# Shifting the start of the product operands inside their slots, in the last feed-forward sub-layer of a diffusion backbone

## The chip, the cores and the metric

The kernel runs on one core of one Trainium2 chip. The metric is the device time of one execution in microseconds, the median of several runs; less is better.

## The reference

The reference is a small diffusion backbone of two layers over 512 latent tokens and 256 context tokens, with a model width of 1024. Each layer is a half-step SwiGLU feed-forward, a token mixer (a short gated convolution in layer 0, grouped-query attention in layer 1), and a second half-step SwiGLU. Every sub-layer starts with an RMSNorm with learned scale and shift and ends in a gated residual. Behind the attention only the latent tokens are still needed, so the last feed-forward sees 512 tokens:

```python
def swiglu(h, w_in, w_out):          # w_in: 1024 x 5632, w_out: 2816 x 1024
    gate, up = jnp.split(h @ w_in, 2, axis=-1)
    return (jax.nn.silu(gate) * up) @ w_out

h = norm_modulate(x_lat, norm_g[i, 2], m_lat[:, 2, 0], m_lat[:, 2, 1])
x_lat = x_lat + 0.5 * m_lat[:, 2, 2] * swiglu(h, ffn_w_in[i, 1], ffn_w_out[i, 1])
...
return rms_norm(x_lat, final_g)
```

## The kernel before

**Arithmetic.** All large products run on TensorE in the type fp32r (four bytes to an element). To keep float32 accuracy every operand is split into a high part, a rounded copy that ScalarE writes, and a low part, the rest, that VectorE writes (`split`, L189 to L191). A product of two operands is then three matmuls, in `mm3` (L863 to L866): weight high by operand high, weight high by operand low, weight low by operand high. Each has its own weight load.

**The first half of a feed-forward.** For each of the 22 chunks of 128 hidden columns, `gate` and `up` are computed from the weights of both (two 128-column blocks, each with its 1024 rows cut in two) and from the normed activations, cut in two over their 1024 rows and in two over their tokens (B11, B21, B12, B22: first index the rows, second the tokens). The first two chunks are computed directly. The other 20 use a scheme with seven products in place of eight (M1 to M7, `PRODUCTS`, L65), which needs sums of the weight blocks and of the operands; the operand sums are T1, T2, T3 and T4. So there are seven operand pairs, each made once for the sub-layer and read by 20 chunks:

```python
PRODUCTS = {"M1": ("A11", "B11", "A"), "M2": ("A12", "B21", "B"), "M3": ("S4", "B22", "C"), "M4": ("A22", "T4", "A"),
            "M5": ("S1", "T1", "C"), "M6": ("S2", "T2", "A"), "M7": ("S3", "T3", "A")}
```

A product is 4 steps over the rows by 3 matmuls, 12 matmuls in all (`product`, L1122 to L1132). In the last sub-layer each half has 256 tokens, so a matmul has 256 columns; in the first three feed-forward and convolution sub-layers it has 384, and the second half of a feed-forward (the operands gh and gl) works on 512. In the round of a chunk the order is M1, M2, M7 of the chunk before, M5, M6, M4 and M3 of the chunk before (`product_order`, L119 to L124), and TensorE follows the order of the program.

**Where the operands lie.** Fourteen slots, tags T0 to T13, are laid out once (`SLOT_ORDER`, L71; L593 to L595). A slot is as large as the largest tile that ever uses its tag: 6144 bytes in a partition (4 x 384 elements), and 6176 for slots 4, 5, 8 and 9, which in the first sub-layers hold B12 and B22 with two more columns. `t_tiles` (L736) puts the high and low part of an operand into two slots, from the first byte of each. In the last sub-layer the slots come from `LAST_T_SLOTS` (L74); B12 and T4 use the same two, one after the other. A tile there is 4 x 256 elements, 4096 bytes, so a part of the slot stays free.

**Where the weights lie.** A weight granule is one tile of 4096 bytes, high part in its first half and low part in its second; eight of them take turns (`place`, L254 to L267). The addresses that the program assigns are these: the granules begin at 96 modulo 256 bytes, the low parts as well; slots 0 to 3, 6 to 8 and 10 to 13 begin at 96, slot 9 at 128, slot 4 at 160, slot 5 at 192 modulo 256.

**Who makes the weights.** Weight blocks come by DMA into raw tiles. For a product, VectorE forms the sum of blocks where one is needed (L374, L383), ScalarE and VectorE split it into a granule (L190, L191), ahead of TensorE as long as granules are free.

Of the kernel before, what the change touches and what calls it, by code (L numbers as in the profile page):

```python
# [26 lines left out]
NH = NT // 2  # L27
# [44 lines left out]
HELD_AFTER_T = ((6, 7), (10, 11), (8, 9))  # L72

LAST_T_SLOTS = {"B11": (0, 1), "B21": (2, 3), "B12": (6, 7), "T4": (6, 7), "T1": (8, 13), "B22": (9, 10), "T2": (11, 12), "T3": (4, 5)}  # L74
LAST_F_SLOTS = {(0, 0): 4, (1, 0): 5, (0, 1): 11, (1, 1): 12}
HELD_AFTER_LAST_T = ((8, 13), (11, 12), (9, 10))
HELD_AFTER_HEADS = ((6, 7), (9, 10))
# [53 lines left out]
def backbone(ctx: ExitStack, tc: tile.TileContext, a: dict, out: bass.AP):  # L131
# [30 lines left out]
    vec, at = {}, 0  # L162
# [23 lines left out]
    def slot(n, shape, name, dt=F32R):  # L186
        return xp.tile([P, *shape], dt, name=name, tag=f"T{n}")
# [410 lines left out]
    hh, hl = [None] * KC, [None] * KC  # L598
# [125 lines left out]
    T, full = {}, {}  # L724
    geo = SimpleNamespace(tokens=TOKENS, half=NH, groups=BOTH, t_slots=T_SLOTS, f_slots=F_SLOTS)
# [8 lines left out]
        region.pop().close()  # L734

    def t_tiles(name, more=0):  # L736
        T[name] = [slot(n, [4, geo.half + more], f"t{name}{z}") for n, z in zip(geo.t_slots[name], "hl")]

    def t_split(name, src, ks, pinned=False):
        split(T[name][0][:, ks], T[name][1][:, ks], src[:, ks], pinned)  # L740
# [12 lines left out]
    def opening(i, s):  # L753
# [27 lines left out]
        def early(half):  # L781

            t_tiles(f"B{half + 1}1")
            off, n = geo.tokens[0]
            for k, (hi, lo) in enumerate(zip(*([t[:, k, :] for k in range(4)] for t in T[f"B{half + 1}1"]))):
                m = 4 * half + k
                scale = scl[:, m, LAT : LAT + 1]
                act.activation(hi, xs(m, off, n), AF.Copy, scale=scale)  # L788
                dve.scalar_tensor_tensor(out=lo, in0=xs(m, off, n), scalar=scale, in1=hi.bitcast(F32), op0=ALU.mult, op1=ALU.subtract)  # L789
# [6 lines left out]
        def parted(half, tok, p, which="both", more=0):  # L796
            name = f"B{half + 1}{tok + 1}"
            if p == 0 and which != "lo":
                t_tiles(name, more)
            hi, lo = T[name][0][:, PAIRS[p], : geo.half], T[name][1][:, PAIRS[p], : geo.half]  # L800
            src = full[half, tok][:, PAIRS[p]]
            if which != "lo":
                act.activation(hi, src, AF.Copy)
            if which != "hi":
                dve.tensor_tensor(out=lo, in0=src, in1=hi.bitcast(F32), op=ALU.subtract)
# [20 lines left out]
        def sum_parted(which, p, pinned=False):  # L826
            if p == 0:
                t_tiles(which)
            t_split(which, full[which] if which in full else full[0, 0], PAIRS[p], pinned)
# [984 lines left out]
    with tc.tile_pool(name="g1", bufs=1) as gp:  # L1814
        stage["ssq"] = lambda: gp.tile([P, NT], F32, name="ssq", tag="ssq")
        heads = attention(gp, 1, 1)
    geo.__dict__.update(tokens=HALVES, half=NL // 2, groups=((0, NL),), t_slots=LAST_T_SLOTS, f_slots=LAST_F_SLOTS)
    op4 = opening(1, 2)
# [79 lines left out]
```

## Time and profile before

| | |
|---|---|
| median of three runs | 2401.55 us (2401.49 to 2401.75) |
| the profiled execution: its own time, its span | 2401.78 us, 2399.9 us |
| granted TensorE clock, mean | 0.999 |
| TensorE matmuls | 14303, busy 99% of the span |
| VectorE, ScalarE | busy 85% and 49% |
| last feed-forward, first half and projections | about 2045 to 2390 us of the span |

Times are microseconds from the start of the span unless marked ns. PE is TensorE's matmul, PEld its weight load, DVE VectorE, ACT ScalarE, POOL GpSimd. L864 to L866 are the three lines of `mm3`, so a matmul is known by its tiles: `ps_A<-tT4h,w` is a matmul into an accumulator of tag A with the high part of T4 as the moving operand and a granule as the weights. Matmuls overlap in the record, and a duration of one is its latency; how fast they follow one another is read from their starts.

### The profile page before, as it was taken

The numbers are of one execution on the slowest core, as the hardware profiler recorded it, in microseconds if no ns is written. First come the engines' busy times: TensorE is split into PE (matmuls) and PEld (weight loads), VectorE is DVE, ScalarE is ACT, GpSimd is POOL, SyncE is SP. The second block draws the span as 40 slices with busy tenths as digits, with TensorE's granted clock in tenths as the row PEclk, the third lists the DMA queues.
The fourth block names the chain that finished last, engine by engine and source line by source line (L and its number), as shares of the span: only waits on it lengthen the run. The fifth ranks groups of instructions, "written<-read, shape, count | busy, mean of one in ns | idle before, by whom it ended". The sixth has DMA issues, their size and how long they took to land.

```text
span 2399.9 us, 37639 instructions
## 1 busy us (share of the span) xinstructions
PE 2379.0 (99%) x14303; PEld 2253.2 (94%) x14303; DVE 2032.3 (85%) x4018; ACT 1166.2 (49%) x2198; POOL 135.4 (6%) x256
## 2 busy tenths in 40 slices
PE   9999999999999999999999999999999999999998
PEld 6999999999999999999999999999998889999998
DVE  6989989978988888888877988788778987987777
ACT  5634334355535553443435544343355776555555
POOL 0001111100000001000000001101100000000000
PEclk9999999999999999999999999999999999999999
DMA  9234334430334123323432144443441101133231
GB/s 338 85 113 140 128 126 132 128 115 27 106 106 132 39 69 116 120 94 118 128 106 67 50 131 128 141 138 122 137 132 54 45 10 58 67 122 95 101 106 62
DMA packets 93062, 253.71 MB, mean 106 GB/s; under 512 B 10320, under 2 KB 18640, under 8 KB 92880
## 3 DMA queue, kind: packets, MB, share of 16 engines
q1 hardware_dynamic: 71984, 183.65, 23.3%
q0 software_dynamic: 20352, 67.12, 8.9%
q8 instruction: 112, 1.84, 0.3%
q14 instruction: 70, 0.57, 0.1%
q10 hardware_dynamic: 544, 0.52, 0.1%
HBM read 249.16 MB, written 2.10 MB: 105 GB/s over the span
## 4 chain that ended last, share of the span: by engine, by line
PE 92%; DVE 3%; ACT 3%; DMA 1%; issue 1%; SPq 0%; DVEq 0%; ACTq 0%
PE ps_A L864 16%; PE ps_A L865 16%; PE ps_A L866 16%; PE ps_C L865 11%; PE ps_C L866 11%; PE ps_C L864 11%; PE ps_B L866 3%; PE ps_B L864 3%; PE ps_B L865 3%; PE ps_T L1545 1%; DMA ada<-in_ada_w 0%; DVE f L766 0%; DMA raw<-in_ffn_w_in 0%; ACT pr L1528 0%; PE ps_O L866 0%
## 5 line engine op out<-in xcount | busy, mean ns | idle before, releaser
L190 ACT ACTIVATE w<-raw 128x512 fp32r<-128x512 f32 (+1 forms) x862 | 522.7, 620 | 716.7 <-PE ps_A L866 224.4
L191 DVE TENSOR_TENSOR w<-raw,w 128x512 fp32r<-128x512 f32 (+1 forms) x862 | 574.1, 679 | 120.0 <-ACT w L190 105.6
L510 POOL DMA_DIRECT2D aw<-in_ada_t x240 | 129.4, 539 | 1368.4 <-DVE mods L531 1100.1
L374 DVE TENSOR_TENSOR raw<-raw,raw 128x512 f32<-128x512 f32 x264 | 181.4, 689 | 8.1 <-DMA raw<-in_ffn_w_in 3.8
L865 PE MATMUL ps_C<-gl,w 128*128 128x512 f32 (+1 forms) x548 | 188.3, 344 | 0.0
L864 PE MATMUL ps_C<-gh,w 128*128 128x512 f32 (+1 forms) x548 | 188.2, 343 | 0.0
L866 PE MATMUL ps_C<-gh,w 128*128 128x512 f32 (+1 forms) x548 | 188.0, 343 | 0.0
L864 PE MATMUL ps_A<-gh,w 128*128 128x512 f32 (+1 forms) x540 | 185.5, 343 | 0.6 <-DVE x L932 0.6
L865 PE MATMUL ps_A<-gl,w 128*128 128x512 f32 (+1 forms) x540 | 185.5, 343 | 0.0
L866 PE MATMUL ps_A<-gh,w 128*128 128x512 f32 (+1 forms) x540 | 185.3, 343 | 0.0
L531 DVE CUSTOM_DVE_ANT_0 ps_S<-aw,silu_row,packed 128x512 f32<-128x512 f32 x208 | 156.9, 754 | 2.2 <-DMA aw<-in_ada_t 0.7
L531 DVE CUSTOM_DVE_ANT_0 ps_S<-aw,silu_row,mods 128x512 f32<-128x512 f32 x208 | 156.8, 754 | 1.0
L932 DVE SCALAR_TENSOR_TENSOR x<-ps_C,gat,x 128x512 f32<-128x512 f32 (+1 forms) x158 | 99.6, 631 | 43.6 <-PE ps_C L866 43.2
L864 PE MATMUL ps_A<-tB11h,w 128*128 128x384 f32 (+1 forms) x400 | 129.9, 325 | 0.2 <-ACT tB11h L788 0.2
L865 PE MATMUL ps_A<-tB11l,w 128*128 128x384 f32 (+1 forms) x400 | 129.5, 324 | 0.2 <-DVE tB11l L789 0.2
L866 PE MATMUL ps_A<-tB11h,w 128*128 128x384 f32 (+1 forms) x400 | 129.3, 323 | 0.0
L865 PE MATMUL ps_C<-tB22l,w 128*128 128x384 f32 (+2 forms) x376 | 121.7, 324 | 0.0
L866 PE MATMUL ps_C<-tB22h,w 128*128 128x384 f32 (+2 forms) x376 | 121.5, 323 | 0.0
L864 PE MATMUL ps_C<-tB22h,w 128*128 128x384 f32 (+2 forms) x376 | 121.2, 322 | 0.0
L932 DVE SCALAR_TENSOR_TENSOR x<-ps_A,gat,x 128x512 f32<-128x512 f32 (+1 forms) x162 | 101.8, 638 | 16.7 <-PE ps_A L866 16.6
L864 PEld LDWEIGHTS ps_A<-gh,w 128*128 128x128 f32 x540 | 102.3, 189 | 14.0 <-issue 1.0
L866 PEld LDWEIGHTS ps_C<-gh,w 128*128 128x128 f32 x548 | 103.8, 189 | 12.3
(486 smaller groups left out, 6939.0 us busy)
## 6 DMA issues: line engine op xcount, KB each, us to landing
raw<-in_ffn_w_in SPq DMA_DIRECT2D x170, 512.0 KB, 3.7
aw<-in_ada_t POOLq DMA_DIRECT2D x240, 256.0 KB, 2.9
raw<-in_ffn_w_out SPq DMA_DIRECT2D x80, 512.0 KB, 4.1
raw<-in_conv_w_in SPq DMA_DIRECT2D x24, 512.0 KB, 3.6
ada<-in_ada_w SPq DMA_DIRECT2D x28, 256.0 KB, 5.4
raw<-in_attn_w_qkv SPq DMA_DIRECT2D x12, 512.0 KB, 5.1
raw<-in_ada_w SPq DMA_DIRECT2D x8, 512.0 KB, 7.1
silu_row<-in_crow POOLq DMA_DIRECT2D x8, 512.0 KB, 3.9
```

The source lines that it names most:

```text
L190: hi = act.activation(dsth, src, AF.Copy)
L191: lo = dve.tensor_tensor(out=dstl, in0=src, in1=dsth.bitcast(F32), op=ALU.subtract)
L374: dve.tensor_tensor(out=quad(o), in0=quad(x), in1=quad(y), op=ALU.subtract)
L510: nc.gpsimd.dma_start(w, a["ada_t"][t, kh, j])
L531: ins = dve.tensor_tensor_reduce(out=junk, in0=w, in1=silu_row[kh][:, v, :], scale=1.0, scalar=total if kh else ada_b[:, i, hm // 2, col : ...
L864: pe.matmul(ps, wh, xh, start=first, stop=False, **kw)
L865: pe.matmul(ps, wh, xl, start=False, stop=False, **kw)
L866: pe.matmul(ps, wl, xh, start=False, stop=last, **kw)
L932: dve.scalar_tensor_tensor(out=x, in0=p[:, o - off : o - off + w], scalar=gat[:, m, v : v + 1], in1=x, op0=ALU.mult, op1=ALU.add)
L1545: pe.transpose(pt[:, c, :], pr[:, (c0 + c) * P : (c0 + c + 1) * P], ident)
```

## The change

In the last sub-layer, which is known by its half of 256 tokens, each operand part now begins some elements inside its slot. The tile is made longer by so many elements and the operand is the rest of it. The numbers in `LAST_T_STARTS` count elements of four bytes, so the starts lie 0 to 192 bytes inside the slots. The earlier sub-layers (`geo.half == NH`) keep the old line. No instruction is added or taken away.

```diff
 LAST_T_SLOTS = {"B11": (0, 1), "B21": (2, 3), "B12": (6, 7), "T4": (6, 7), "T1": (8, 13), "B22": (9, 10), "T2": (11, 12), "T3": (4, 5)}
+LAST_T_STARTS = {"B11": (16, 32), "B21": (16, 16), "B12": (32, 16), "T4": (32, 16), "T1": (16, 48), "B22": (0, 16), "T2": (16, 32), "T3": (16, 24)}
...
     def t_tiles(name, more=0):
-        T[name] = [slot(n, [4, geo.half + more], f"t{name}{z}") for n, z in zip(geo.t_slots[name], "hl")]
+        if geo.half == NH:
+            T[name] = [slot(n, [4, geo.half + more], f"t{name}{z}") for n, z in zip(geo.t_slots[name], "hl")]
+            return
+        T[name] = []
+        for n, z, at in zip(geo.t_slots[name], "hl", LAST_T_STARTS[name]):
+            t = slot(n, [at + 4 * geo.half], f"t{name}{z}")
+            T[name].append(t[:, at:].rearrange("p (k c) -> p k c", k=4))
```

## The prediction

> **What bounds the kernel now.** I read the page first: how busy TensorE is, and whose work the chain that ended last consists of.
>
> ```profile
> PE 2379.0 (99%) x14303; PEld 2253.2 (94%) x14303; DVE 2032.3 (85%) x4018; ACT 1166.2 (49%) x2198; POOL 135.4 (6%) x256
> ...
> PE 92%; DVE 3%; ACT 3%; DMA 1%; issue 1%; SPq 0%; DVEq 0%; ACTq 0%
> ```
>
> TensorE is busy 99% of the span and carries 92% of the chain. So what counts is not a wait but how closely one matmul follows another. Second, the busy times by stretch, for the last feed-forward sub-layer: the rounds of products begin near 2061 us, and the last of them ends near 2366 us. Columns: length, then busy time and count of PE, PEld, DVE, ACT, POOL, the granted clock, DMA share, GB/s.
>
> ```profile
> 2061.00:2100.00 39.00, 37.28 (x261) 34.37 (x260) 38.12 (x72) 22.15 (x52) 0.00 (x0) 1.00 0.23 82
> 2100.00:2366.00 266.00, 266.00 (x1885) 250.94 (x1884) 215.27 (x389) 140.90 (x284) 0.00 (x0) 1.00 0.31 102
> ```
>
> Up to 2100 us it is VectorE that is full (38.12 of 39.00) and TensorE has holes. From 2100 to 2366 us TensorE has none (266.00 of 266.00), VectorE is 81% busy, ScalarE 53%, the granted clock is 1.00. Third, the waits in that second stretch; the longest sum is ScalarE's, which waits with a weight split until TensorE gives a granule back:
>
> ```profile
> ACT w L190 <- PE ps_C L866: 31.4, 19, 4.7
> ```
>
> So weights lie ready ahead of TensorE, and a faster TensorE is fed. Fourth, the timeline of TensorE, for the spacing of the matmuls. A matmul's own duration here (0.28) is its latency; the pace is the distance of starts. Shown is the first matmul of six products, in one round of seven; each product has 12 matmuls of 256 columns.
>
> ```profile
> 2146.73 0.28 PE L864 MATMUL ps_B<-tB21h,w 128*128 128x256 f32 x1
> ...
> 2148.17 0.28 PE L864 MATMUL ps_A<-tT3h,w 128*128 128x256 f32 x1
> ...
> 2149.59 0.28 PE L864 MATMUL ps_C<-tT1h,w 128*128 128x256 f32 x1
> ...
> 2152.46 0.28 PE L864 MATMUL ps_A<-tT4h,w 128*128 128x256 f32 x1
> ...
> 2153.90 0.28 PE L864 MATMUL ps_C<-tB22h,w 128*128 128x256 f32 x1
> ...
> 2155.32 0.28 PE L864 MATMUL ps_A<-tB11h,w 128*128 128x256 f32 x1
> ...
> 2156.76 0.28 PE L864 MATMUL ps_B<-tB21h,w 128*128 128x256 f32 x1
> ```
>
> B21, T4 and B11 take 1.44 us for 12 (120.0 ns each). T3 (2148.17 to 2149.59) and B22 (2153.90 to 2155.32) take 1.42 (118.3 ns). T1 and T2 together take 2.87. The round of 84 takes 10.03, or 119.4 ns each. These seven products do the same work; what separates T3 and B22 is where their operands lie. Every weight tile of this sub-layer begins at the same residue of 256 bytes. Four slots of the first sub-layers are 32 bytes longer (the two added columns of B12 and B22, in slots 4, 5, 8, 9), which pushes slot 9 by 32, slot 4 by 64 and slot 5 by 96 bytes against the weights; all others stand at 0. B22 (slots 9, 10) is thus at 32 and 0, T3 (slots 4, 5) at 64 and 96, and the five others at 0 and 0. Both displaced pairs are the quicker ones.
>
> **The change, part by part.** No instruction, wait, transfer or slot is added, removed or moved. Only first bytes move: `at` counts four-byte elements, so the starts are 0 to 192 bytes inside the slots. Distances (high, low part) from the weights' residue become: B11 64, 128; B21 64, 64; T4 and B12 128, 64; T1 64, 192; T2 64, 128; B22 32, 64; T3 128, 192.
>
> Writing the operands: ScalarE and VectorE write at other starts. The trace has such a pair already, B22 against B21:
>
> ```profile
> L805 DVE TENSOR_TENSOR tB22l<-f,tB22h 128x512 fp32r<-128x512 f32 x2 | 1.4, 688 | 0.3 <-ACT tB22h L803 0.3
> L805 DVE TENSOR_TENSOR tB21l<-f,tB21h 128x512 fp32r<-128x512 f32 x2 | 1.4, 686 | 0.0
> ```
>
> The displaced one costs 2 ns more; there are 32 such writes (eight pairs in two halves, by two engines), at most 0.1 us, and I take nothing. If that cover is gone it falls into the stretch before 2100 us, where VectorE is full.
>
> Reading them: the number of matmuls that can gain. The groups by line, from 2100 to 2366 us:
>
> ```profile
> L864 PE MATMUL ps_A<-tT4h,w 128*128 128x256 f32 x76 | 21.5, 283 | 0.0
> ...
> L864 PE MATMUL ps_A<-tB11h,w 128*128 128x256 f32 x68 | 19.2, 282 | 0.0
> ```
>
> Between 68 and 76 for each operand and line, and 1494 for all seven operands and three lines, or 17.8 rounds of 84. The 186 that run before 2100 us I count at nothing: there VectorE sets the pace, and TensorE's gain would become waiting (at the same 2 ns they would be 0.4 us).
>
> The price of a new distance has no row of its own, so I bound it. At the same width there is one more displaced case, the held weights at the end, whose high half lies 32 bytes off:
>
> ```profile
> 2374.03 0.28 PE L864 MATMUL ps_A<-gh,f12held 128*128 128x256 f32 x1
> ...
> 2376.86 0.28 PE L864 MATMUL ps_C<-gh,f12held 128*128 128x256 f32 x1
> ```
>
> 24 matmuls in 2.83 us, 117.9 ns each. For other widths there are these, first 512 columns:
>
> ```profile
> 2137.13 0.39 PE L864 MATMUL ps_A<-gh,w 128*128 128x512 f32 x1
> ...
> 2142.57 0.39 PE L864 MATMUL ps_C<-gh,w 128*128 128x512 f32 x1
> ```
> ```profile
> 1830.95 0.39 PE L864 MATMUL ps_A<-h,w 128*128 128x512 f32 x1
> ...
> 1836.50 0.40 PE L864 MATMUL ps_B<-h,w 128*128 128x512 f32 x1
> ```
>
> In both, 24 matmuls: 5.44 us (226.7 ns) with all operands at distance 0, and 5.55 us (231.3 ns) where the low parts lie in slots 4, 5, 8 and 9, at 64, 96, 0 and 32. Here displacement costs 4.6 ns. And 384 columns, an earlier sub-layer with T4 in slots 4 and 5 (64, 96):
>
> ```profile
> 1753.02 0.33 PE L864 MATMUL ps_A<-tT2h,w 128*128 128x384 f32 x1
> ...
> 1755.10 0.33 PE L864 MATMUL ps_A<-tT4h,w 128*128 128x384 f32 x1
> ...
> 1757.20 0.34 PE L864 MATMUL ps_C<-tB22h,w 128*128 128x384 f32 x1
> ```
>
> T2 at 0 takes 2.08 us (173.3 ns), T4 takes 2.10 (175.0). So distance matters at every width, and its sign depends on the width: -1.7 to -2.1 ns at 256, +1.7 at 384, +4.6 at 512.
>
> The ends: for the better, from 226.7 and 120.0 a column costs (226.7 - 120.0) / 256 = 0.417 ns, so 256 columns are 106.7 ns and 13.3 ns are left over in each matmul at distance 0. That remainder gone whole would be 1494 x (119.4 - 106.7) = 19.0 us, but the three displaced cases took only 13% to 16% of it. For the worse, 4.6 ns as at 512 columns: 1494 x 4.6 = 6.9 us lost. I go by the rows of the same width: all three gained. I take 1.41 us for each of the seven products (117.5 ns), a shade under the 1.415 of the held weights, since both 1.42 cases hold an odd multiple of 32 bytes, which after the change only B22 does. A round is then 9.87 us instead of 10.03, and 17.8 rounds save 0.16 each, 2.85 us.
>
> The other work: the projections out of the sub-layer (gh, gl) and the tail after 2366 us keep their addresses. What is late next: if TensorE runs 1.3% faster, VectorE goes from 81% to 82%, so nothing.
>
> The sum against the profiled execution: span 2399.9 - 2.85 = 2397.05, with the 1.9 us around it 2398.9 instead of 2401.78. The median of the three runs is 2401.55, 0.23 lower, so I forecast 2398.7 us.
>
> **The rivals.** First: the distances do more. Three cases are few, and what is left of the 13.3 ns is 11 ns. Were twice as much taken, 4 ns from the matmuls now at 120.0 (115.9 ns for all, say), the gain is 1494 x 3.5 = 5.2 us: 2396.3. With 5 ns off the mean of 119.4 it is 7.5 us: 2394.1. For it speaks that T1 gains right after T3 although its own distance is 0 (T1 and T2 take 2.87, not 2.88), so runs of mixed distances hold short steps; against it, that no product in the trace is under 1.415.
>
> Second: nothing happens. If only the distance within 64 bytes mattered, the five pairs at 0 stay at 120.0, since all their new distances are multiples of 64, B22 keeps its 32, and T3 loses its 96: 18 x 0.02 = 0.4 us lost, 2401.9. The row against it is T3's: its high part stands at 64, its low part at 96, and I can't part the two there. [...]
>
> Third, the other side: the new distances act at 256 columns as displacement does at 384 and 512. In five pairs high and low part now stand at different distances, as in the 231.3 ns case, where the distance changes from matmul to matmul. At +1.7 ns it is 1494 x 1.7 = 2.5 us lost (2404.1), at +4.6 ns 6.9 us (2408.4). It decides against me from a mean spacing of 119.4 ns on, and shows as slower from 122.6 ns on (4.8 us over 1494). For it: T4 at 384 and the 512-column row. Against it: B22 and T3 alternate too, at this width, and gain.
>
> **How the numbers follow.** 0.2% of 2401.55 is 4.8 us, about what a measurement of this kernel can tell from no change; that is 3.2 ns for each of 1494 matmuls. The forecast's case (0.5 to 4.8 us gained, spacing 119.1 to 116.2) gets 0.61; the first rival (over 4.8) 0.27; the second (within 0.5) 0.07; the third 0.05, of which 0.04 beyond 4.8 us. So faster 0.27, same 0.61 + 0.07 + 0.01 = 0.69, slower 0.04. The range goes from 2395.4 (6.15 us gained, 115.3 ns), into the first rival, to 2401.6, which takes in most of the second; about 0.08 lie under it and 0.10 over it.
>
> **What would show it.** In the timeline after: a product of 12 at 1.41 for B11, B21, T1, T2, T4 (now 1.44), a round at 9.87 (now 10.03), the gh run of 24 at 5.44 as before, everything up to about 2010 us in its place, and the end earlier by 2.9 us. Rounds of 10.03 would show the second rival, over 10.03 the third, under 9.76 the first. The prediction is wrong beyond that if TensorE shows new holes between 2100 and 2366 us, or if ScalarE and VectorE take up another order of instructions.

## The result, and the profile after

The changed kernel takes 2398.9 us, median of 21 runs (2398.11 to 2399.52); the kernel before takes 2401.75 us in as many runs beside it. That is 2.85 us less. The ratio is 0.9987, with a 95% interval of 0.9981 to 0.9993. The profiled execution took 2398.45 us, with a span of 2396.6 us.

The page of the changed kernel, engine totals, and the busy times of the two stretches (columns as before):

```profile
PE 2375.8 (99%) x14303; PEld 2250.3 (94%) x14303; DVE 2031.6 (85%) x4018; ACT 1165.9 (49%) x2198; POOL 135.1 (6%) x256
```
```profile
2061.00:2100.00 39.00, 37.23 (x263) 34.27 (x262) 38.27 (x72) 22.30 (x51) 0.00 (x0) 1.00 0.26 84
2100.00:2362.00 262.00, 262.00 (x1872) 246.96 (x1871) 213.44 (x386) 139.51 (x282) 0.00 (x0) 1.00 0.32 103
```

The counts of instructions are the same, TensorE still has no hole from 2100 us on, and its busy time fell by 3.2 us. On each engine the instructions stand in the same order, but for one VectorE memset of 59 ns near 725 us, long before the changed sub-layer, which trades places with its neighbour. So the time is a matter of pace alone. Here is one round in the timeline of TensorE; the lines of `mm3` are now L871 to L873, and the start is the first column:

```profile
2145.52 0.28 PE L871 MATMUL ps_B<-tB21h,w 128*128 128x256 f32 x1
...
2146.94 0.28 PE L871 MATMUL ps_A<-tT3h,w 128*128 128x256 f32 x1
...
2148.36 0.28 PE L871 MATMUL ps_C<-tT1h,w 128*128 128x256 f32 x1
...
2149.78 0.28 PE L871 MATMUL ps_A<-tT2h,w 128*128 128x256 f32 x1
...
2151.19 0.28 PE L871 MATMUL ps_A<-tT4h,w 128*128 128x256 f32 x1
...
2152.58 0.28 PE L871 MATMUL ps_C<-tB22h,w 128*128 128x256 f32 x1
...
2153.99 0.28 PE L871 MATMUL ps_A<-tB11h,w 128*128 128x256 f32 x1
...
2155.41 0.28 PE L871 MATMUL ps_B<-tB21h,w 128*128 128x256 f32 x1
```

The round takes 9.89 us instead of 10.03. B21, T1, T2, B22 and B11 take 1.41 to 1.42 for 12 matmuls, T3 still takes 1.42, and T4 only 1.39.

Where the time came off is read from the starts of the same matmuls in both traces, first of the kernel before, then of the changed one. They are the first matmul with an operand of the last sub-layer, the first product of the rounds, the start of the full stretch, and, for the changed kernel, a matmul behind the last product:

```profile
2039.09 0.28 PE L864 MATMUL ps_A<-tB11h,w 128*128 128x256 f32 x1
...
2063.71 0.28 PE L864 MATMUL ps_A<-tB11h,w 128*128 128x256 f32 x1
...
2100.58 0.28 PE L864 MATMUL ps_A<-tT4h,w 128*128 128x256 f32 x1
```
```profile
2038.66 0.28 PE L871 MATMUL ps_A<-tB11h,w 128*128 128x256 f32 x1
...
2063.12 0.28 PE L871 MATMUL ps_A<-tB11h,w 128*128 128x256 f32 x1
...
2099.74 0.28 PE L871 MATMUL ps_A<-tT4h,w 128*128 128x256 f32 x1
...
2370.70 0.28 PE L871 MATMUL ps_A<-gh,f12held 128*128 128x256 f32 x1
```

The changed kernel is 0.43, 0.59 and 0.84 us ahead at the first three, and 3.33 us at the last, which stood at 2374.03 before. The 0.43 arose ahead of the changed sub-layer and is the difference of two executions. The two directly computed chunks brought 0.16 us, the VectorE-bound rounds up to 2100 us 0.25 us, the full stretch after them 2.49 us, and the tail nothing. That is 2.90 us in all.

### The profile page after: what moved, and what is told of

Read it like the earlier page. It is cut to its first block, busy times and chain, and to the rows that moved or that the text cites. A ratio compares the mean times of both kernels' runs of the same rounds, so it can differ in the third digit from the quotient of the medians.

```text
span 2396.6 us, 37639 instructions
## 1 busy us (share of the span) xinstructions
PE 2375.8 (99%) x14303; PEld 2250.3 (94%) x14303; DVE 2031.6 (85%) x4018; ACT 1165.9 (49%) x2198; POOL 135.1 (6%) x256
## 4 chain that ended last, share of the span: by engine, by line
PE 91%; DVE 3%; ACT 2%; DMA 2%; issue 1%; SPq 0%; DVEq 0%; ACTq 0%
PE ps_A L871 16%; PE ps_A L872 16%; PE ps_A L873 16%; PE ps_C L872 11%; PE ps_C L873 11%; PE ps_C L871 11%; PE ps_B L873 3%; PE ps_B L872 3%; PE ps_B L871 3%; DMA ada<-in_ada_w 1%; DMA x<-in_x 1%; PE ps_T L1552 1%; DVE f L773 0%; ACT pr L1535 0%; PE ps_O L873 0%
## 5 line engine op out<-in xcount | busy, mean ns | idle before, releaser
L871 PE MATMUL ps_C<-gh,w 128*128 128x512 f32 (+1 forms) x548 | 188.2, 343 | 0.0
L873 PE MATMUL ps_C<-gh,w 128*128 128x512 f32 (+1 forms) x548 | 188.0, 343 | 0.0
L871 PE MATMUL ps_A<-gh,w 128*128 128x512 f32 (+1 forms) x540 | 185.5, 344 | 0.6 <-DVE x L939 0.6
L873 PE MATMUL ps_A<-gh,w 128*128 128x512 f32 (+1 forms) x540 | 185.3, 343 | 0.0
L871 PE MATMUL ps_A<-tB11h,w 128*128 128x384 f32 (+1 forms) x400 | 129.6, 324 | 0.2 <-ACT tB11h L795 0.2
L873 PE MATMUL ps_A<-tB11h,w 128*128 128x384 f32 (+1 forms) x400 | 129.0, 323 | 0.0
L873 PE MATMUL ps_C<-tB22h,w 128*128 128x384 f32 (+2 forms) x376 | 121.5, 323 | 0.0
L871 PE MATMUL ps_C<-tB22h,w 128*128 128x384 f32 (+2 forms) x376 | 121.1, 322 | 0.0
L871 PEld LDWEIGHTS ps_A<-gh,w 128*128 128x128 f32 x540 | 102.3, 189 | 14.0 <-issue 1.0
L873 PEld LDWEIGHTS ps_C<-gh,w 128*128 128x128 f32 x548 | 103.8, 189 | 12.3
```

What stands on the lines that cost most here:

```text
L871: pe.matmul(ps, wh, xh, start=first, stop=False, **kw)
L873: pe.matmul(ps, wl, xh, start=False, stop=last, **kw)
```

## The experiments

All of these change where operands start, and nothing in what is computed. A distance is meant against the weights' residue, modulo 256 bytes, high part first. The times of single products are medians over the rounds from 2097 us on, from the starts in the timeline. "Pace" is the mean step from one matmul's start to the next.

**All pairs at 64, 64.** The starts are chosen so that every pair has B21's distances:

```diff
-LAST_T_STARTS = {"B11": (16, 32), "B21": (16, 16), "B12": (32, 16), "T4": (32, 16), "T1": (16, 48), "B22": (0, 16), "T2": (16, 32), "T3": (16, 24)}
+LAST_T_STARTS = {"B11": (16, 16), "B21": (16, 16), "B12": (16, 16), "T4": (16, 16), "T1": (16, 16), "B22": (8, 16), "T2": (16, 16), "T3": (0, 56)}
```

> All seven pairs at 64 and 64 bytes against the weights. Theory (the pace of a pair is set by its own distance from the weights): every product as B21 has it after the change, 12 matmuls in 1.413 us (117.8 ns), a round of 84 in 9.89 us, the whole about 2399.0 us. Rival (a gain needs high and low part at different distances, and B21 gains only because its neighbours do): steady 1.44 us per product as at distance 0, 2402.5 us.

2398.75 us, ratio to the kernel before 0.9988 (0.9979 to 0.9997). All seven products take 1.413 to 1.414 us (117.8 ns a matmul). Two rows of the timeline, one round apart:

```profile
2146.07 0.28 PE L871 MATMUL ps_B<-tB21h,w 128*128 128x256 f32 x1
...
2155.97 0.28 PE L871 MATMUL ps_B<-tB21h,w 128*128 128x256 f32 x1
```

9.90 us, as the theory has it. High and low part need not differ, and distances that are multiples of 64 do count, against my second rival. The same distance also has a quicker pace, though only for a short while: from 2046.51 to 2050.25 us, 33 matmuls of the directly computed chunks took 3.74 us, 113.3 ns each.

**All pairs at 128, 64**, the distances of T4:

```diff
+LAST_T_STARTS = {"B11": (32, 16), "B21": (32, 16), "B12": (32, 16), "T4": (32, 16), "T1": (32, 16), "B22": (24, 16), "T2": (32, 16), "T3": (16, 56)}
```

> All seven pairs at 128 and 64, the distances at which T4 runs at 116.1 ns after the change. Theory (a pair's distances alone set its pace): all seven products at about 1.393 us, a round in 9.75 us, the whole about 2396.5 us. Rival (T4 is quick because of its place in the round, behind T2 and into the same kind of accumulator): T4 stays near 1.39, the others stay near 1.415, about 2399 us.

2398.16 us, 0.9985 (0.9976 to 0.9994). All seven take 1.405 to 1.406 us by the median, T4 too. Neither theory holds: the distances alone don't set the pace, and T4's place in the round doesn't either. What ran before does count: ahead of the first projection of 512 columns in the stretch, the 23 products from 2090.8 us on take 1.426 or 1.427 us each, and behind it nearly all take 1.401 to 1.408. One round of each:

```profile
2103.60 0.28 PE L871 MATMUL ps_A<-tB11h,w 128*128 128x256 f32 x1
...
2113.59 0.28 PE L871 MATMUL ps_A<-tB11h,w 128*128 128x256 f32 x1
```
```profile
2145.37 0.28 PE L871 MATMUL ps_A<-tB11h,w 128*128 128x256 f32 x1
...
2155.20 0.28 PE L871 MATMUL ps_A<-tB11h,w 128*128 128x256 f32 x1
```

**All pairs at 0.**

```diff
+LAST_T_STARTS = {"B11": (0, 0), "B21": (0, 0), "B12": (0, 0), "T4": (0, 0), "T1": (0, 0), "B22": (56, 0), "T2": (0, 0), "T3": (48, 40)}
```

> B22 and T3 too are put at distance 0 (modulo 256 bytes), so that nothing is displaced. Theory: every product 1.44 us (120.0 ns), a round in 10.08 us, about 0.9 us slower than the kernel before: 2402.6 us. Rival (whole multiples of 256 are not the same as 0, or B22 and T3 are quicker for another reason, such as their place in the round): B22 and T3 keep 1.42 us and the time stays at 2401.7.

2402.74 us, 1.0003 (0.9994 to 1.0013): 0.96 us over the kernel before. Every product takes 1.440 us, also B22 and T3 at 256 instead of 0:

```profile
2147.54 0.28 PE L871 MATMUL ps_B<-tB21h,w 128*128 128x256 f32 x1
...
2157.62 0.28 PE L871 MATMUL ps_B<-tB21h,w 128*128 128x256 f32 x1
```

10.08 us for a round. That the kernel before had 10.03 it owed to the accident of the four longer slots.

**Weights moved with the operands.** The starts of the first experiment, and 64 bytes ahead of the granules:

```diff
+    nc.vector.memset(tmp.tile([P, 16], F32, name="pad", tag="pad", bufs=1), 0.0)
```

> As the first run, but 64 bytes are also put ahead of all weight granules, so that the operands of the last sub-layer lie where they lay in the first run and are at distance 0 from the weights again. Theory (distance to the weights): 1.44 us per product in the last sub-layer. Rival (the operand's own place): 1.413 us as in the first run. The shift also puts most products of 384 columns, in the earlier sub-layers, at a distance of 192: by the row of T4 at 384 columns they would take 2.10 us instead of 2.08, which over about 500 products is 10 us lost, 2412 us in all; if they gain as the 256-column ones do (2 ns each of some 5000) it is 10 us won, 2392 us.

2410.8 us, 1.0037 (1.0024 to 1.0051). The operands lie where they lay in the first experiment, and the products are back at 1.440 us. What counts, for these shifts of 64 bytes, is the distance between the two streams, not where the operand lies. The earlier sub-layers' products, now at 192:

```profile
1758.30 0.34 PE L873 MATMUL ps_A<-tT3h,w 128*128 128x384 f32 x1
...
1760.40 0.34 PE L873 MATMUL ps_C<-tT1h,w 128*128 128x384 f32 x1
...
1762.50 0.33 PE L873 MATMUL ps_A<-tT2h,w 128*128 128x384 f32 x1
```

2.10 us instead of 2.08: at 384 columns this displacement costs. Summed over their starts in both traces, the matmuls of 384 columns make 8.8 of the 9 us that this run lost.

**Four surveys**, in each of which every pair has its own distance. Equal distances first:

```diff
+LAST_T_STARTS = {"B11": (8, 8), "B21": (24, 24), "B12": (56, 56), "T4": (56, 56), "T1": (40, 40), "B22": (4, 12), "T2": (48, 48), "T3": (16, 8)}
```

> A survey: each pair has high and low part at one distance of its own: B11 32, B21 96, T3 128, T1 160, T2 192, T4 224, B22 48. Theory 1 (two streams that share one place at distance 0 and not otherwise): every product at 1.413 us as at 64, 64. Theory 2 (the distance acts with a period of 128 bytes): T3 at 128 takes 1.44 us, T2 at 192 and B21 at 96 stay under 1.42.

Then small and large ones:

```diff
+LAST_T_STARTS = {"B11": (1, 1), "B21": (2, 2), "B12": (20, 20), "T4": (20, 20), "T1": (6, 6), "B22": (20, 28), "T2": (256, 256), "T3": (52, 44)}
```

> A survey of small and of large distances, high and low part alike: B11 4, B21 8, T3 16, T1 24, T4 80, B22 112, T2 1024. If what counts is which 64-byte line a read falls into, B11 to T1 (4 to 24 bytes) take 1.44 us and T4 and B22 1.413; if it is a 16-byte line, B11 and B21 take 1.44 and T3 and T1 1.413. T2 at 1024 takes 1.44 in either case, since only the distance within 256 bytes has counted so far.

And unequal ones:

```diff
+LAST_T_STARTS = {"B11": (0, 32), "B21": (32, 0), "B12": (24, 8), "T4": (24, 8), "T1": (16, 0), "B22": (40, 32), "T2": (0, 16), "T3": (32, 56)}
```

> A survey of unequal distances: B11 0, 128; B21 128, 0; T3 192, 64; T1 64, 0; T2 0, 64; T4 96, 32; B22 192, 128. Theory (only equal distances hold one steady pace, unequal ones lie between 1.39 and 1.43, without a rule that the distances alone give): the seven spread over at least 0.02 us. Rival (the pace is the mean of what the three matmuls have at their own distances, 120.0 at 0 and 117.8 else): B11, B21, T1 and T2 between 1.42 and 1.43, T3, T4 and B22 at 1.413.

The last survey, made after the run with all pairs at 112 (below), fills the gaps around it:

```diff
+LAST_T_STARTS = {"B11": (60, 60), "B21": (36, 36), "B12": (30, 30), "T4": (30, 30), "T1": (52, 52), "B22": (20, 28), "T2": (26, 26), "T3": (28, 20)}
```

> A survey around 112 and of the odd multiples of 16 bytes not tried yet, high and low part alike: B11 240, B21 144, T3 176, T1 208, T2 104, T4 120, B22 112. Theory (one lucky distance): only B22 falls to 1.36 us, and within its 12 matmuls; the others lie between 1.40 and 1.44, T2 and T4 higher, since they are no multiples of 16. Rival (period 128, or every odd multiple of 16 from 112 on): B11 at 240, which is 112 + 128, takes 1.36 as well.

Each was run once: 2399.03, 2401.32, 2399.46 and 2400.06 us. Product lengths, in us; but for the two marked "all pairs" each is taken behind a pair with another distance, so it is no steady pace (all pairs at 192 give 1.360 or 1.413 below, all at 112 give 1.360):

```
equal, multiples of 16   0: 1.440 (all pairs)   16: 1.403   32: 1.414   48: 1.418   64: 1.413 (all pairs)
                         80: 1.428   96: 1.440   112: 1.398 and 1.406   128: 1.423   144: 1.423   160: 1.410
                         176: 1.426   192: 1.381   208: 1.416   224: 1.414   240: 1.410   1024: 1.429
equal, others            4: 1.475   8: 1.453   24: 1.440   104: 1.438   120: 1.443
unequal                  0,128: 1.413   128,0: 1.408   192,64: 1.417   64,0: 1.419   0,64: 1.414   96,32: 1.414   192,128: 1.428
```

None of the simple rules holds. 128 isn't 0 (1.423), 240 isn't 112, and 96 is no better than 0. Neither prediction came true, that for 64 bytes or that for 16: 4 and 8 (1.475, 1.453) are worse than 0, 16 (1.403) is better, 24 (1.440) is not. Two rows show B11 at 4 bytes, the slowest, in 1.48 us:

```profile
2145.01 0.28 PE L871 MATMUL ps_A<-tB11h,w 128*128 128x256 f32 x1
...
2146.49 0.28 PE L871 MATMUL ps_B<-tB21h,w 128*128 128x256 f32 x1
```

What stays is coarser: all five distances that are no multiple of 16 take 1.438 us or more, and of the multiples only 0 and 96 do. Since the weights begin at a multiple of 16, these five are also the operands that begin off such a multiple; no run tells whether the distance or the operand's own start counts here. Nor does any run show why these five are slow (1.438 to 1.475 us), or what orders the multiples of 16 (1.381 to 1.440 us). The seven unequal ones spread from 1.408 to 1.428, as the theory had it. Among them the mean of the single distances fails too: 0,128 and 128,0 beat what it gave (1.42 to 1.43), and 192,128 is slower. And 1024 was still at 1.429, where the steady pace of 0 is 1.440. A product that keeps some of what came before it would explain that; no run puts all pairs at 1024 to show it. 112 in a mixed round reached its quick steps only in its last matmuls and came out at 1.398 and 1.406, not at the 1.36 I had expected of it in the last survey.

**Taking turns.** 64, 128 and 128, 64 alternate through the round:

```diff
+LAST_T_STARTS = {"B11": (16, 32), "B21": (32, 16), "B12": (32, 16), "T4": (32, 16), "T1": (32, 16), "B22": (8, 32), "T2": (16, 32), "T3": (0, 8)}
```

> The seven pairs take turns: 64, 128 and 128, 64 (B21, T1 and T4 have the latter). Theory (the pace depends on the state that the product before leaves: T4 at 128, 64 behind T2 at 64, 128 takes 1.391 us after the change, and 1.405 where all pairs are at 128, 64): B21, T1 and T4 take 1.391, the four others 1.415; a round 9.83 us, against 9.84 for all at 128, 64; the whole about 2398.2 us. Rival (T4's 1.391 belongs to its place in the round): only T4 takes 1.391, the other two 1.405; a round 9.86.

2397.71 us, 0.9983 (0.9973 to 0.9993). Its timeline:

```profile
2146.64 0.28 PE L871 MATMUL ps_B<-tB21h,w 128*128 128x256 f32 x1
...
2148.03 0.28 PE L871 MATMUL ps_A<-tT3h,w 128*128 128x256 f32 x1
...
2149.44 0.28 PE L871 MATMUL ps_C<-tT1h,w 128*128 128x256 f32 x1
...
2150.83 0.28 PE L871 MATMUL ps_A<-tT2h,w 128*128 128x256 f32 x1
```

B21, T1 and (by the median) T4 take 1.391 us behind a pair at 64, 128, and the others 1.409 to 1.413. So the pace of a product depends on what the product before it leaves, which I call its state, and T4's quick 1.39 in the changed kernel comes from T2 ahead of it.

**All pairs at 192, 192**, the quickest of the surveys:

```diff
+LAST_T_STARTS = {"B11": (48, 48), "B21": (48, 48), "B12": (48, 48), "T4": (48, 48), "T1": (48, 48), "B22": (40, 48), "T2": (48, 48), "T3": (32, 24)}
```

> All seven pairs at 192 and 192. In the survey T2 at 192, 192 went, after three matmuls of 118 to 123 ns, to 114 to 115 ns in each of the other nine. Theory (that is the steady pace of this distance, and what stood before it is forgotten within a product): all seven products at about 1.37 us (114.3 ns), a round 9.60 us, the whole about 2393.5 us, 5.4 less than the changed kernel. Rival (a passing state, as with T4 at 128, 64, that pays back in longer runs): about 1.41 per product, 2399 us.

2397.53 us, 0.9983 (0.9974 to 0.9992). Both were half right. One round before the first projection of the stage, and one after it:

```profile
2093.83 0.28 PE L871 MATMUL ps_B<-tB21h,w 128*128 128x256 f32 x1
...
2103.35 0.28 PE L871 MATMUL ps_B<-tB21h,w 128*128 128x256 f32 x1
```
```profile
2144.22 0.28 PE L871 MATMUL ps_B<-tB21h,w 128*128 128x256 f32 x1
...
2154.11 0.28 PE L871 MATMUL ps_B<-tB21h,w 128*128 128x256 f32 x1
```

9.52 us (113.3 ns a matmul), then 9.89 (117.7 ns), with the same operands at the same distances. The first state holds through 23 products until the 512-column projection ends it. The second then holds almost to the end, where one late step stands ahead of a return to the first:

```profile
2357.90 0.31 PE L871 MATMUL ps_A<-tT4h,w 128*128 128x256 f32 x1
2358.05 0.28 PE L872 MATMUL ps_A<-tT4l,w 128*128 128x256 f32 x1
2358.17 0.28 PE L873 MATMUL ps_A<-tT4h,w 128*128 128x256 f32 x1
```

Up to here the steps are 117 to 119 ns, this one is 151 ns, and the 23 matmuls behind it go at 113 to 114 ns. So the state can also change at a single late step, with no other width or distance in between.

**All pairs at 112, 112.**

```diff
+LAST_T_STARTS = {"B11": (28, 28), "B21": (28, 28), "B12": (28, 28), "T4": (28, 28), "T1": (28, 28), "B22": (20, 28), "T2": (28, 28), "T3": (12, 4)}
```

> All seven pairs at 112 and 112. In the survey B22 at 112, 112 ended on four matmuls of 113 to 114 ns. Theory (steady at 114 ns, as with 192): products at 1.37 us, about 2393.5 us. Rival (112 is no multiple of 32, and the short steps are paid back by steps of 119 to 120 as in the first eight): about 1.40 per product, 2397.5 us.

2391.96 us, 0.9959 (0.9946 to 0.9973): 9.7 us under the kernel before, 6.9 under the changed one, and the best version found.

```profile
2144.54 0.28 PE L871 MATMUL ps_B<-tB21h,w 128*128 128x256 f32 x1
...
2154.06 0.28 PE L871 MATMUL ps_B<-tB21h,w 128*128 128x256 f32 x1
```
```profile
2100.00:2355.00 255.00, 255.00 (x1863) 239.76 (x1863) 211.43 (x385) 137.61 (x281) 0.00 (x0) 1.00 0.32 106
```

9.52 us a round. Behind a projection, at 112, B11 needs nine matmuls of 114 to 121 ns until the 113.3 ns are there; after that they stay until the next projection. TensorE shows no hole even at this pace (255.00 of 255.00), and VectorE is at 83%. But a matmul's record lasts 0.28 us, so the busy time hides a wait shorter than that: near 2352.7 us two steps took 256 and 227 ns, where a weight load waited 0.2 us for VectorE to read out an accumulator (L1156). The kernel before and the changed one have no such wait in their full stretch.

**112 at other widths.** On top of the version above, the projections' operands and T1 of the earlier sub-layers:

```diff
-            t = gp.tile([P, per, width], F32R, name=f"g{z}{f}", tag=tags(z, f // per))
+            t = gp.tile([P, 64 + per * width], ...)[:, 28 : 28 + per * width].rearrange("p (k c) -> p k c", k=per) if width == NL else ...
...
+            if name == "T1":
+                T[name] = [slot(n, [64 + 4 * NH], f"t{name}{z}")[:, 28 : 28 + 4 * NH].rearrange("p (k c) -> p k c", k=4) for ...]
```

> As the run with all seven pairs at 112, and 112 also at two other widths: the operands gh and gl of the last sub-layer's projections (512 columns) and T1 of the earlier sub-layers (384 columns; its two slots grow by 256 bytes). Theory (at distance 112 a matmul has 272 cycles for 256 columns instead of 288, so 16 cycles of overhead instead of 32, at any width): 220.0 ns instead of 226.7 at 512 columns, 166.7 instead of 173.3 at 384; 384 x 6.7 ns + 816 x 6.7 ns = 8 us less than 2392.0, so 2384 us. Rival (which distance is good depends on the width, as 192 is good at 256 columns and bad at 384): 231 ns and 175 ns or so, 2395 us.

A cycle there is the 0.417 ns that a column costs by the steps of 120.0 ns at 256 columns and 226.7 at 512; 113.3 ns are about 272 of them, 120.0 ns 288.

2394.67 us, 0.997 (0.9959 to 0.9981), 2.7 us worse than without it (2.4 us when each is held against the kernel before timed beside it). The rival holds: 12 matmuls of 512 columns take 2.77 us (230.8 ns) instead of 2.72,

```profile
2133.91 0.39 PE L874 MATMUL ps_C<-gh,w 128*128 128x512 f32 x1
...
2136.68 0.39 PE L874 MATMUL ps_A<-gh,w 128*128 128x512 f32 x1
```

and T1 at 384 columns takes 2.09 us where 0 has 2.08, with T2 behind it, still at 0, at 2.10.

## Why the prediction was right, point by point

The prediction was 2398.7 us against 2398.9 measured, and the mechanism was the one it named, the distance between operand and weights. That the pace also depends on what ran before was not in it. Two terms of its sum were off, in opposite directions: 2.49 us instead of 2.85 in the full stretch, and 0.41 us instead of nothing ahead of it. That they nearly cancel, to 2.90, is luck.

- *What bounds.* Right. TensorE's pace passed into the end without a loss: 2.49 us came off in the stretch without holes, and the tail moved by the same amount. No engine became late in the changed kernel; at 113.3 ns VectorE did once, by 0.2 us.
- *What separates T3 and B22 from the others is their distance from the weights.* Right. All at 0 brings both to 1.440 us, and moving the weights along takes the gain away again: 1.440 us, with the operands where they had taken 1.413.
- *The gain per round, 0.16 us.* Measured 0.14, and 17.8 rounds of it are the 2.49 us. The flat 1.41 us for each product was a mean over unlike values: T4 took 1.39, B21, T2 and B22 1.413, T1 and B11 1.415 to 1.416, and T3 1.425, no better than the 1.422 it had. The reason given for going under 1.415, that an odd multiple of 32 bytes is the worse distance, fails: T3 has none any more and is the slowest, and B11 at 32, 32 took 1.414 in the survey.
- *The matmuls before 2100 us gain nothing.* Wrong: the rounds there gained 0.25 us, of the 0.4 that I had put beside it as the price without cover. VectorE was busy 38.12 of 39.00 us, yet TensorE's gain was not all turned into waiting. Another 0.16 us came from the two directly computed chunks, from 2039 us on, which also read B11 to B22 and stand in no term of the sum. No run shows how the gain gets past VectorE there.
- *Writes at displaced starts cost nothing.* Right: the low part of B22 takes 689 ns after, 688 before; that of B21, now displaced as well, takes 682 after, 686 before.

```profile
L812 DVE TENSOR_TENSOR tB22l<-f,tB22h 128x512 fp32r<-128x512 f32 x2 | 1.4, 689 | 0.3 <-ACT tB22h L810 0.3
...
L812 DVE TENSOR_TENSOR tB21l<-f,tB21h 128x512 fp32r<-128x512 f32 x2 | 1.4, 682 | 0.0
```

- *First rival, the distances do more.* Not so for the distances of this change. But it was right about what was to be had: all pairs at 112 gain 9.7 us, more than the case that I worked out. What spoke for it, T1 gaining behind T3 with its own distance at 0 (1.432 us by the median in the kernel before), was the first sign of the states: with all pairs at 0, T1 takes 1.440 us too.
- *Second rival, nothing happens.* Refuted by the run at 64, 64: 117.8 ns, against 120.0 at distance 0, for the same work.
- *Third rival, slower as at 384 and 512 columns.* Refuted at 256 columns, by every multiple of 16 that was tried but 96, which took the 1.440 us of 0; at the two other widths the distances tried cost time (2.09 and 2.10 us instead of 2.08 at 384 columns, 2.77 instead of 2.72 at 512). One reading in it is off: after the change six of the seven pairs have high and low part at different distances, all but B21, and not five.

## What to carry to other kernels

Where TensorE has no holes and each matmul loads new weights, as here (14303 loads to 14303 matmuls), look at the step from one matmul's start to the next, not at durations: the residue of the moving operand's address against the weights' changes it by some 6% at 256 columns (113.3 ns with all pairs at 112, 120.0 at 0), for no instruction and a few bytes. Try the distances on the chip for each width, with all operands at the same one, and judge by whole rounds behind whatever comes before them; a survey within one kernel mixes the states (112 took 1.398 and 1.406 us there, and 1.360 with all pairs at it). Don't transfer a good distance from one width to another: at 512 columns 112 took 230.8 ns, and 0 took 226.7.

## What the runs showed of the hardware that I had not expected

- At distance 0 the steps of the kernel before are 120.0, 173.3 and 226.7 ns at 256, 384 and 512 columns. By my estimate from these three they are 0.417 ns a column and 13.3 ns on top, the time of 32 columns. At 256 columns and distance 112 the step is 113.3 ns, which by the same estimate leaves only 6.7, the time of 16 columns.
- The pace has a memory. At 192, the same stream runs steadily at 113.3 or at 117.7 ns, by the state in which it was entered, and holds it through whole products; 64 has shown both paces too (113.3 and 117.8), and 128, 64 has shown 118.9 and 117.0. At 112 it fell into the quick state by itself, within about a dozen matmuls. Why is open: the runs show what the pace depends on, not what in the hardware brings it about.
- The five distances tried that are no multiple of 16 bytes are among the worst (1.438 to 1.475 us for a product, against 1.440 at 0).
